# State rows of a streaming convolution moved through small contiguous tiles, and one buffer of the norm's mean in place of two

## The chip, the cores and the metric

One core of one Trainium2 chip runs the whole program. The metric is the device time of one execution in microseconds (us), as the median of several runs. TensorE does the matrix products, VectorE and GpSimd the elementwise work, ScalarE activations and copies, and all transfers between HBM and on-chip memory (SBUF) are issued on SyncE, whose queue the profile calls SPq. TensorE writes to PSUM banks.

## What is computed

Two layers of a streaming encoder, in float32, on 512 prompt frames and 64 frames of a running stream side by side (T = 576 columns, 1,024 features). The part that the change touches is the convolution branch of each layer and the norms. The reference, cut:

```python
def conv_mixer(u, conv_state, conv_w, conv_b, ln_g, ln_b):
    full = jnp.concatenate([conv_state.astype(u.dtype), u], axis=1)
    y = lax.conv_general_dilated(full, conv_w[:, None, :], ..., feature_group_count=C_CONV) + conv_b
    y = jax.nn.silu(layer_norm(y, ln_g, ln_b))
    return y, full[:, -(CONV_WIDTH - 1):]       # the last 30 rows are the new state, an output
...
    h = x @ w_in
    a, g, q, k, v, qi, ki, wi = jnp.split(h, points, axis=-1)
    u = a * jax.nn.sigmoid(g)
    conv_out, new_conv = conv_mixer(u, conv_state, conv_w, conv_b, cln_g, cln_b)
    ...                                         # rope, indexer scores, top-k, attention
    mix = jnp.concatenate([conv_out, attn_out], axis=-1) @ w_o
    x = layer_norm(ALPHA * x + mix, ln1_g, ln1_b)
    gate, up = jnp.split(x @ w_gate_up, 2, axis=-1)
    x = layer_norm(ALPHA * x + (jax.nn.silu(gate) * up) @ w_down, ln2_g, ln2_b)
```

The state goes in for the running stream (`state_conv`), and out for both groups (`new_conv_p`, `new_conv_s`).

## The kernel before, in words

Features lie on the 128 partitions, frames along the free dimension, in two halves of 288 columns. Each weight tile is loaded (`raw`, two buffers), split by ScalarE into a high part (`whi`) and by VectorE or GpSimd into a low part (`wlo`), and a product is three float32r matmuls per block (`products`, `weight`, line 443). 

A layer runs: the products of the convolution's gate and value, the indexer queries and keys with their rotary embedding (`rope`: ScalarE copies the product out of PSUM into `rope_h`, four transfers swap the half heads into `rope_s`, VectorE and GpSimd multiply, VectorE adds), the scores and a top-k by repeated max and replace on VectorE, then keys, values and queries, attention over five query tiles, the convolution's norm, the output projection with its norm, and the feed-forward part with its norm.

The convolution works on four units of 128 channels (`glu(c, ...)`, line 720, c = 0 to 3). The unit's input `u` is a tile of 128 partitions x 8 phases x 80 columns, frame t at phase t mod 8: in each phase 4 columns of zeros, 64 of the prompt, 4 of the old state (from `I_S`) and 8 of the running stream. `glu` clears the zeros on GpSimd, loads the state columns from `st[l, c]` straight into `u`, lets VectorE write gate times value, and stores two pieces of 4 columns per phase to `conv_p` and `conv_s`. The tensors in HBM hold 128 x 8 x 4 numbers without gaps; in `u` each run of 4 numbers (16 B) is followed by a gap. Then `convolve(c)` (line 654) stores all of `u` to a scratch tensor in HBM (`ud<-u`), loads it back with phases on partitions (`v<-ud`, 8 transfers of 16 partitions), builds the tap matrices on GpSimd (`taps`), runs 80 matmuls, and `convolved` (line 679) sends the result back in the same manner (`yd<-y`, `c<-yd`). Units 0 and 1 are made at the head of the layer, units 2 and 3 after the scores.

A norm (`Sums.norm`, line 551) is done for each half of the columns: sums over features on TensorE, then ScalarE spreads the negated mean (`nmu`) and the inverse deviation (`rstd`) over the partitions, VectorE adds and multiplies for eight blocks. Both tiles come from `tmp` (line 421) with two buffers. The tail of the attention's last query tile uses the tag `nmu` too (`ptn`, line 949).

The order of the work is not that of the program text. Every operation is first recorded with a priority, and a planner (`schedule`, line 253) then lays out the whole program as a list on a modelled clock: of the ready operations of an engine it takes the one of lowest priority number, buffers are handed out and freed on that clock, and each engine's instructions, those of the DMA-issuing queue too, stand in that order on the chip, where an instruction that waits holds all behind it. The planner's model prices a transfer by bytes alone, at 360 bytes a nanosecond after a fixed delay, and does not know the size of its pieces; a transfer is issued only when the modelled backlog of DMA is under 3 us. A GpSimd copy of n columns is priced at 0.15 us and 0.0033 us a column. `convolve(c)` has priority CONV + 1000 c, ahead of what comes later in the layer.

```python
            nc.sync.dma_start(u[:, :, I_S:I_S + PADS], ins["st"][l, c])            # line 723
            nc.sync.dma_start(outs["conv_p"][l, c], u[:, :, I_S - PADS:I_S])       # line 731
            nc.sync.dma_start(outs["conv_s"][l, c], u[:, :, CIN - PADS:])          # line 732
```

Of the kernel before, what the change touches and what calls it, by code (L numbers as in the profile page):

```python
# [11 lines left out]
F32 = mybir.dt.float32  # L12
# [5 lines left out]
P = 128  # L18
# [5 lines left out]
HT = T // 2  # L24
# [25 lines left out]
PH = 8  # L50
CB = P // PH
PADS = 32 // PH
CIN = (NP + NS) // PH + 2 * PADS
COUT = CIN - PADS
CJ = 40 // PH
I_S = NP // PH + PADS
# [309 lines left out]
def stream_step(ctx, tc, ins, outs):  # L366
    ctx.enter_context(tc.nc.allow_low_precision(reason="float32r parts"))
    nc = Plan(tc)
# [5 lines left out]
    small = nc.pool(ctx, "small", 4)  # L374
# [28 lines left out]
    def f(x):  # L403
        return x.bitcast(F32)
# [3 lines left out]
    def bank(name, tag="b"):  # L408
        return pb.tile([P, 512], F32, tag=tag, name=name, bufs=BANKS[tag])
# [11 lines left out]
    def tmp(name, tag, n=T, bufs=2):  # L421
        return work.tile([P, n], F32, tag=tag, name=name, bufs=bufs)
# [103 lines left out]
    class Sums:  # L526
# [23 lines left out]

        def norm(self, prm, og, ob, h, last):
            x = lambda k: X[:, k, H[h]]
            nmu, rstd = dst = [tmp(x, x, HT) for x in ("nmu", "rstd")]
            mo = Moments(self.s1[:, H[h]], self.s2[:, H[h]], D, HT, 3, dst)
            mo.stats()
            mo.spread(0)
            mo.spread(1)
            for k in range(KD):
                nc.vector.tensor_add(x(k), x(k), nmu)
                nc.vector.tensor_mul(x(k), x(k), rstd)  # L560
                nc.scalar.activation(x(k), x(k), AF.Identity, scale=prm[:, og + k:og + k + 1],
                                     bias=prm[:, ob + k:ob + k + 1])
                if last:
                    nc.sync.dma_start(outs["y"][:, k, H[h]], x(k))
                else:
                    nc.scalar.activation(XH[:, k, H[h]], x(k), AF.Copy)
                    nc.vector.tensor_sub(XL[:, k, H[h]], x(k), f(XH[:, k, H[h]]))
# [75 lines left out]
    def layer(l):  # L643
# [10 lines left out]
        def convolve(c):  # L654
            wv = slot.tile([P, PH, CJ * PH], F32, tag="wv", name="wv")
            nc.sync.dma_start(wv, ins["cw"][l, c])
            v = slot.tile([P, PH, CIN], F32, tag=f"c{c}", name=f"v{c}")
            ud = dram.tile([P, PH, CIN], F32, tag="ud", name="ud")
            nc.sync.dma_start(ud, us[c])
            for q in range(PH):  # L660
                nc.sync.dma_start(v[q * CB:(q + 1) * CB], ud[:, q, :].rearrange("(b c) t -> c b t", c=CB))
            ps = wide("conv")
            for b in range(PH):
                sw = tmp("taps", "tap", CJ * P)
                shape = [P, CJ * PH, CB]
                nc.gpsimd.tensor_mul(sw.rearrange("p (a b) -> p a b", b=CB), eyes.unsqueeze(1).to_broadcast(shape),
                                     wv[:, b, :].unsqueeze(2).to_broadcast(shape))
                o = b % 4 * COUT
                for j in range(CJ):
                    nc.tensor.matmul(ps[:, b // 4, o:o + COUT], sw[:, j * P:(j + 1) * P], v[:, b, j:j + COUT],  # L670
                                     start=(j == 0), stop=(j == CJ - 1))
            y = slot.tile([P, PH, COUT], F32, tag=f"u{c}", name=f"y{c}")
            for h in range(2):
                nc.vector.tensor_add(y[:, 4 * h:4 * h + 4, :], ps[:, h, :4 * COUT].rearrange("p (b t) -> p b t", b=4),
                                     prm[0][:, O_CB + c * PH + 4 * h:O_CB + c * PH + 4 * h + 4].unsqueeze(2)
                                     .to_broadcast([P, 4, COUT]))
            convolved(c, y)
# [42 lines left out]
        def glu(c, pg, pa):  # L720
            u = slot.tile([P, PH, CIN], F32, tag=f"u{c}", name=f"u{c}")
            nc.gpsimd.memset(u[:, :, 0:PADS], 0.0)
            nc.sync.dma_start(u[:, :, I_S:I_S + PADS], ins["st"][l, c])
            sg = tmp("sg", "sg")
            for h in range(2):
                nc.scalar.activation(sg[:, H[h]], pg[h][:, :HT], AF.Sigmoid)
            for i, h, a, n in ((PADS, 0, 0, HT), (PADS + HT // PH, 1, HT, NP - HT), (I_S + PADS, 1, NP, NS)):
                step = lambda x: x.rearrange("p (t s) -> p t s", s=PH)
                nc.vector.tensor_mul(u[:, :, i:i + n // PH].rearrange("p s t -> p t s"),
                                     step(pa[h][:, a - h * HT:a - h * HT + n]), step(sg[:, a:a + n]))  # L730
            nc.sync.dma_start(outs["conv_p"][l, c], u[:, :, I_S - PADS:I_S])
            nc.sync.dma_start(outs["conv_s"][l, c], u[:, :, CIN - PADS:])
            us.append(u)
            with at(base + CONV + 1000 * c):
                convolve(c)

# [200 lines left out]
        def values(t, u, pr):  # L937
            s = (t + 1) * P if t < 4 else PAST + NS
            sums, _, o = state_[t]
            pt = tmp("pt", "pt", CC)  # L940
            pp = bank("pp", "p")
            nb = min(t + 1, 4)
            for b in range(nb):
                nc.tensor.transpose(pp[:, b * P:(b + 1) * P], pr[:, b * P:(b + 1) * P], ident)
            nc.scalar.activation(pt[:, :nb * P], pp[:, :nb * P], AF.Copy)
            if t == 4:
                pn = bank("pp", "p")
                nc.tensor.transpose(pn[:NS, :P], pr[:, PAST:s], ident)
                ptn = tmp("ptn", "nmu", HT)[:, :P]
                nc.scalar.activation(ptn[:NS], pn[:NS, :P], AF.Copy)  # L950
            d = HD if t < 4 else P
            if u % 4 == 0:
                state_["po"] = bank("po")
            pv = state_["po"][:, (u % 4) * d:(u % 4 + 1) * d]
            gd = slice(u // 4 * HD, (u // 4 + 1) * HD) if t < 4 else slice(0, P)
            for b in range(nb):
                nc.tensor.matmul(pv, pt[:, b * P:(b + 1) * P], (vt if t < 4 else vp)[:, b, gd],
                                 start=(b == 0), stop=(b == t))
            if t == 4:
                nc.tensor.matmul(pv, ptn[:NS], vt[:NS, 4, :], start=False, stop=True)  # L960
            if u % 4 != 3:
                return
            po = state_["po"]
            rs = small.tile([P, 4], F32, tag="rs", name="rs", bufs=2)
            nc.vector.reciprocal(rs, sums[:, u - 3:u + 1])
            if t < 4:
                g = u // 4
                nc.vector.tensor_mul(
                    o[:, g * 256:(g + 1) * 256].rearrange("p (b e d) -> p e b d", b=2, e=2),
                    po[:, :4 * HD].rearrange("p (e b d) -> p e b d", e=2, d=HD),  # L970
                    rs.rearrange("p (e b) -> p e b", e=2).unsqueeze(3).to_broadcast([P, 2, 2, HD]))
                if g == 0:
                    return
                n, no = P, 4
            else:
                po = po.rearrange("p (u g d) -> p u g d", g=2, d=HD)
                for g in range(2):
                    nc.vector.tensor_mul(
                        o[:, g * P:(g + 1) * P].rearrange("p (u d) -> p u d", u=2), po[:, 2 * g:2 * g + 2, g, :],
                        rs[:, 2 * g:2 * g + 2].unsqueeze(2).to_broadcast([P, 2, HD]))  # L980
                n, no = NS, 2
            pm = bank("otr")
            for i in range(no):
                nc.tensor.transpose(pm[:, i * P:(i + 1) * P], o[:, i * P:(i + 1) * P], ident)
            src = pm[:, :4 * n].rearrange("p (i q) -> p i q", i=4)
            hi, lo = XH[:, 4:8, t * P:t * P + n], XL[:, 4:8, t * P:t * P + n]
            nc.scalar.activation(hi, src, AF.Copy)
            nc.vector.tensor_sub(lo, src, f(hi))

        def attend(ts):  # L990
            units = [(t, u) for t in ts for u in range(NH if t < 4 else NH // 2)]
            ahead = []
            for t, u in units:
                ahead.append((t, u, logits(t, u)))
                if len(ahead) > 2:
                    values(*ahead.pop(0))
            for x in ahead:
                values(*x)
# [9 lines left out]
        nmu, rstd = [tmp(x, "tap", UW)[:, :CWID] for x in ("cnmu", "crstd")]  # L1008
# [143 lines left out]
        for part, nf in enumerate(PARTS):  # L1152
# [35 lines left out]
            for j in range(j0, nf):  # L1188
                s = Seven(l, f0 + j, ops)
# [13 lines left out]
            if part < len(PARTS) - 1:  # L1203
                for m in range(KD):
                    ps = products([weight(ins[f"w_d{part}"][l, m], nf * P)], hs)[0]
                    for h in range(2):
                        x = X[:, m, H[h]]
# [115 lines left out]
```

## Time and profile before

| | |
|---|---|
| median of 3 runs | 1572.07 us (1569.68 to 1573.81) |
| profiled execution, its own time | 1578.27 us |
| its span, first to last instruction | 1576.5 us |
| TensorE busy | 1466.2 us (93%) |
| VectorE busy | 1096.8 us (70%) |
| ScalarE busy | 721.0 us (46%) |
| GpSimd busy | 484.3 us (31%) |
| mean granted clock of TensorE | 0.926 of full speed |
| DMA packets | 87,712, of them 49,441 under 512 B |

Busy time is the time in which an engine ran instructions; the rest it waited. Names as `ud<-u` read "written from read". All rows of the trace stand under one line of the code (362), that of the helper that issues the planned list, so operations are told apart by their tiles. A wait is put down to what ended it.

### The profile page before, as it was taken

Reading aid. Unit: us, or ns where it says so; the run is one execution under the profiler, and the core shown is the slowest. Engines: PE = TensorE matmul, PEld = TensorE weight load, DVE = VectorE, ACT = ScalarE, POOL = GpSimd, SP = SyncE. Lnnn points to the kernel's source line nnn. Section 1 sums busy time; section 2 is a strip of 40 time slices with the busy share of each in tenths; the row PEclk is TensorE's granted clock in tenths of the full one; section 3 lists DMA queues with packets and bytes.
Section 4 is the critical chain, followed back from the end, with each engine's and each line's share of the span. In section 5 each row is a group of like instructions: output and inputs, shape, how many; then the busy total and the mean of one; then the engine's idle time right before and its main releaser. Section 6 shows DMA issues by size and latency. Waiting matters only on the chain.

```text
span 1576.5 us, 26565 instructions
## 1 busy us (share of the span) xinstructions
PE 1466.2 (93%) x10246; PEld 1427.4 (91%) x10246; DVE 1096.8 (70%) x2040; ACT 721.0 (46%) x1421; POOL 484.3 (31%) x413
## 2 busy tenths in 40 slices
PE   5799899898999999999996998989989999999996
PEld 5789888898899999999995988979979999999996
DVE  3359878456868668577764989764586785775875
ACT  3334344643635435346453434446364452552643
POOL 1030456333213203122611316533431141230343
PEclk9979959698999999999998997877989999999997
DMA  6625411011132222223327362200112222232221
GB/s 190 121 76 78 118 55 37 14 51 45 54 107 91 88 82 97 90 92 94 99 43 139 73 107 69 68 16 28 55 43 85 101 95 93 81 98 91 78 71 61
DMA packets 87712, 125.12 MB, mean 79 GB/s; under 512 B 49441, under 2 KB 55713, under 8 KB 87585
## 3 DMA queue, kind: packets, MB, share of 16 engines
q1 hardware_dynamic: 87584, 123.42, 28.2%
q8 instruction: 80, 1.31, 0.3%
q14 instruction: 48, 0.39, 0.1%
HBM read 108.81 MB, written 9.21 MB: 75 GB/s over the span
## 4 chain that ended last, share of the span: by engine, by line
PE 74%; DVE 13%; DMA 5%; ACT 3%; SPq 2%; issue 2%; POOL 1%; ACTq 0%; DVEq 0%; POOLq 0%
PE prod L362 30%; PE q L362 16%; PE r L362 8%; PE conv L362 5%; PE c L362 4%; PE po L362 3%; DVE X L362 3%; DMA ud<-u 2%; SPq L362 2%; DVE sel L362 2%; PE qk L362 2%; DVE wlo L362 2%; DVE rope_h L362 2%; PE pp L362 2%; PE dots L362 2%
## 5 line engine op out<-in xcount | busy, mean ns | idle before, releaser
L362 PE MATMUL prod<-XH,whi 128*128 128x288 f32 (+2 forms) x928 | 290.7, 319 | 45.6 <-ACT rope_h L362 25.4
L362 DVE TENSOR_TENSOR wlo<-raw,whi 128x512 fp32r<-128x512 f32 (+2 forms) x199 | 248.4, 1249 | 119.3 <-ACT whi L362 117.3
L362 ACT ACTIVATE whi<-raw 128x1024 fp32r<-128x1024 f32 (+2 forms) x206 | 183.0, 889 | 287.7 <-PE prod L362 174.3
L362 PE MATMUL prod<-XH,wlo 128*128 128x288 f32 (+2 forms) x928 | 290.3, 315 | 7.4 <-DVE wlo L362 7.4
L362 PE MATMUL prod<-XL,whi 128*128 128x288 f32 (+2 forms) x928 | 291.8, 316 | 2.8 <-DVE XL L362 2.7
L362 PEld LDWEIGHTS prod<-XH,whi 128*128 128x128 f32 (+1 forms) x928 | 183.3, 200 | 52.0 <-ACT rope_h L362 27.1
L362 PE MATMUL prod<-hl,whi 128*128 128x288 f32 x704 | 208.0, 296 | 0.2
L362 PE MATMUL prod<-hh,wlo 128*128 128x288 f32 x704 | 207.7, 296 | 0.0
L362 PE MATMUL prod<-hh,whi 128*128 128x288 f32 x704 | 207.0, 295 | 0.0
L362 PEld LDWEIGHTS prod<-XH,wlo 128*128 128x128 f32 (+1 forms) x928 | 182.1, 197 | 10.6 <-DVE wlo L362 8.4
L362 PEld LDWEIGHTS prod<-XL,whi 128*128 128x128 f32 (+1 forms) x928 | 183.8, 198 | 8.2 <-DVE XL L362 6.1
L362 ACT ACTIVATE whi<-s 128x512 fp32r<-128x512 f32 x160 | 96.4, 626 | 134.9 <-PE q L362 101.8
L362 DVE TENSOR_TENSOR wlo<-s,whi 128x512 fp32r<-128x512 f32 x158 | 107.3, 700 | 65.3 <-ACT whi L362 64.3
L362 PE MATMUL q<-XH,wlo 128*128 128x288 f32 x480 | 141.2, 295 | 1.5 <-DVE wlo L362 1.3
L362 PE MATMUL q<-XL,whi 128*128 128x288 f32 x480 | 141.4, 295 | 0.0
L362 PE MATMUL q<-XH,whi 128*128 128x288 f32 x480 | 141.3, 294 | 0.0
L362 PEld LDWEIGHTS prod<-hl,whi 128*128 128x128 f32 x704 | 132.1, 188 | 1.0 <-DVE hl L362 0.7
L362 PEld LDWEIGHTS prod<-hh,wlo 128*128 128x128 f32 x704 | 132.0, 188 | 0.1
L362 PEld LDWEIGHTS prod<-hh,whi 128*128 128x128 f32 x704 | 131.9, 188 | 0.2
L362 POOL TENSOR_TENSOR s<-raw 128x512 f32<-128x512 f32 x28 | 44.9, 1607 | 248.6 <-DVE wlo L362 210.6
L362 POOL TENSOR_TENSOR taps<-eyes,wv 128x640 f32<-128x640 f32 x64 | 87.4, 1369 | 91.1 <-PE conv L362 60.8
L362 DVE TENSOR_TENSOR X<-X,prod 128x288 f32<-128x288 f32 x120 | 53.1, 449 | 86.1 <-PE prod L362 85.5
(195 smaller groups left out, 3537.1 us busy)
## 6 DMA issues: line engine op xcount, KB each, us to landing
raw<-in_w_u SPq DMA_DIRECT2D x44, 512.0 KB, 3.2
raw<-in_w_g SPq DMA_DIRECT2D x44, 512.0 KB, 3.2
raw<-in_w_in SPq DMA_DIRECT2D x36, 512.0 KB, 4.3
raw<-in_w_d SPq DMA_DIRECT2D x48, 384.0 KB, 3.0
raw<-in_w_o SPq DMA_DIRECT2D x16, 512.0 KB, 3.3
raw<-in_w_d SPq DMA_DIRECT2D x16, 256.0 KB, 2.7
rope_s<-rope_h SPq DMA_DIRECT2D x48, 72.0 KB, 2.0
ud<-u SPq DMA_DIRECT2D x8, 320.0 KB, 9.6
```

What stands on the lines that cost most here:

```text
L362: getattr(engine, op.method)(*map(take, op.args), **{k: take(v) for k, v in op.kw.items()})
```

## The change

The state rows are loaded into a small tile `cin` (128 x 32 numbers, one buffer for all units) and copied into `u` by GpSimd; what is stored is first copied by GpSimd out of `u` into a small tile `cout` (two buffers) and stored from there. On both sides of the transfers each partition's 32 numbers are then one run of 128 B. The recording of the two stores also moves behind the line that hands `u` to `convolve`. The mean of the norm gets one buffer instead of two, and with it `ptn`.

```diff
         def norm(self, prm, og, ob, h, last):
-            nmu, rstd = dst = [tmp(x, x, HT) for x in ("nmu", "rstd")]
+            nmu, rstd = dst = [tmp(x, x, HT, n) for x, n in (("nmu", 1), ("rstd", 2))]
...
         def glu(c, pg, pa):
             u = slot.tile([P, PH, CIN], F32, tag=f"u{c}", name=f"u{c}")
             nc.gpsimd.memset(u[:, :, 0:PADS], 0.0)
-            nc.sync.dma_start(u[:, :, I_S:I_S + PADS], ins["st"][l, c])
+            row = small.tile([P, PH * PADS], F32, tag="cin", name="cin", bufs=1)
+            nc.sync.dma_start(row, ins["st"][l, c].rearrange("p s t -> p (s t)"))
+            nc.gpsimd.tensor_copy(u[:, :, I_S:I_S + PADS], row.rearrange("p (s t) -> p s t", s=PH))
...
-            nc.sync.dma_start(outs["conv_p"][l, c], u[:, :, I_S - PADS:I_S])
-            nc.sync.dma_start(outs["conv_s"][l, c], u[:, :, CIN - PADS:])
             us.append(u)
+            for name, i in (("conv_p", I_S - PADS), ("conv_s", CIN - PADS)):
+                row = small.tile([P, PH * PADS], F32, tag="cout", name="cout", bufs=2)
+                nc.gpsimd.tensor_copy(row.rearrange("p (s t) -> p s t", s=PH), u[:, :, i:i + PADS])
+                nc.sync.dma_start(outs[name][l, c].rearrange("p s t -> p (s t)"), row)
             with at(base + CONV + 1000 * c):
                 convolve(c)
...
-                ptn = tmp("ptn", "nmu", HT)[:, :P]
+                ptn = tmp("ptn", "nmu", HT, 1)[:, :P]
```

## Rows read from the trace of the kernel before

**Rows 1.** The page, part 2: forty equal slices (39.4 us each) of the span, counted from 0; busy tenths of TensorE and of the DMA engines.

```profile
PE   5799899898999999999996998989989999999996
...
DMA  6625411011132222223327362200112222232221
```

**Rows 2.** The page: packets of all DMA queues.

```profile
DMA packets 87712, 125.12 MB, mean 79 GB/s; under 512 B 49441, under 2 KB 55713, under 8 KB 87585
```

**Rows 3.** The DMA view: issues by kind, count, KB each, median us from issue to landing.

```profile
raw<-in_w_in SPq DMA_DIRECT2D x36, 512.0 KB, 4.3
...
ud<-u SPq DMA_DIRECT2D x8, 320.0 KB, 9.6
v<-ud SPq DMA_DIRECT2D x64, 40.0 KB, 2.0
yd<-y SPq DMA_DIRECT2D x8, 304.0 KB, 2.2
...
u<-in_st SPq DMA_DIRECT2D x8, 16.0 KB, 2.9
```

**Rows 4.** The timeline of the DMA-issuing queue (SPq), unit 2 of layer 1: start us, us on the queue, operation.

```profile
901.29 0.61 SPq L362 DMA_DIRECT2D out_conv_p<-u  x1
901.99 0.63 SPq L362 DMA_DIRECT2D out_conv_s<-u  x1
```

**Rows 5.** Windows over two neighbouring stretches: stretch, us, then busy us of PE, PEld, DVE, ACT, POOL (with counts), granted clock, DMA share, GB/s.

```profile
901.00:912.00 11.00, 11.00 (x67) 9.92 (x66) 10.61 (x24) 4.92 (x14) 0.00 (x0) 1.00 0.87 71
912.00:921.00 9.00, 9.00 (x68) 8.91 (x67) 8.75 (x20) 4.26 (x7) 2.73 (x3) 1.00 0.37 108
```

**Rows 6.** The timeline of the same queue, units 0 and 3 of layer 0.

```profile
44.80 0.43 SPq L362 DMA_DIRECT2D ud<-u  x1
50.27 0.33 SPq L362 DMA_DIRECT2D raw<-in_w_in  x1
...
55.58 7.85 SPq L362 DMA_DIRECT2D v<-ud  x8
...
64.68 2.52 SPq L362 DMA_DIRECT2D rope_s<-rope_h  x4
...
160.12 2.21 SPq L362 DMA_DIRECT2D v<-ud  x5
162.44 2.48 SPq L362 DMA_DIRECT2D rope_s<-rope_h  x4
```

**Rows 7.** The timeline of ScalarE in layer 0: in brackets the idle time before and what ended it.

```profile
62.04 1.06 ACT L362 ACTIVATE whi<-raw 128x1024 fp32r<-128x1024 f32 x1 [6.30 <-DMA raw<-in_w_in]
```

**Rows 8.** Waits of TensorE from 52 to 100 us: us in total, times, longest.

```profile
PE prod L362 <- ACT rope_h L362: 9.4, 2, 5.8
```

**Rows 9.** The timeline of the DMA-issuing queue, units 0 and 1 of layer 1.

```profile
819.30 0.92 SPq L362 DMA_DIRECT2D out_conv_p<-u  x1
...
841.60 0.32 SPq L362 DMA_DIRECT2D v<-ud  x1
```

**Rows 10.** Waits of TensorE from 810 to 880 us.

```profile
PE prod L362 <- ACT rope_h L362: 8.0, 2, 6.7
PE dots L362 <- DMA rope_s<-rope_h: 5.8, 1, 5.8
```

**Rows 11.** Windows of layer 0, columns as in rows 5: a stretch with waits, the making of units 0 and 1, that of units 2 and 3.

```profile
60.00:110.00 50.00, 37.42 (x197) 35.09 (x198) 28.43 (x41) 18.35 (x39) 16.59 (x12) 0.78 0.43 114
...
40.00:60.00 20.00, 19.98 (x126) 18.94 (x124) 6.08 (x9) 4.19 (x6) 0.00 (x0) 1.00 0.69 88
...
120.00:160.00 40.00, 40.00 (x274) 38.30 (x273) 38.50 (x97) 17.63 (x37) 3.79 (x5) 1.00 0.59 75
```

**Rows 12.** The timeline of VectorE before the keys' rope in layer 0 and in layer 1.

```profile
168.49 0.76 DVE L362 TENSOR_TENSOR rope_h<-rope_h,cos 128x576 f32<-128x576 f32 x1 [7.69 <-DMA rope_s<-rope_h]
...
940.10 0.76 DVE L362 TENSOR_TENSOR rope_h<-rope_h,cos 128x576 f32<-128x576 f32 x1 [6.27 <-DMA rope_s<-rope_h]
```

**Rows 13.** The timeline of the DMA-issuing queue at the start.

```profile
10.04 1.41 SPq L362 DMA_DIRECT2D u<-in_st  x2
...
17.84 0.83 SPq L362 DMA_DIRECT2D raw<-in_w_in  x2
```

**Rows 14.** A group of GpSimd by form: count | busy us, mean ns | idle before.

```profile
L362 POOL CAST qi<-bias 128x64 fp32r<-128x64 f32 x16 | 4.9, 352 | 1.0 <-PE prod L362 1.0
```

**Rows 15.** The timelines of VectorE (the same multiply twice) and of GpSimd (the multiply beside the first).

```profile
189.60 1.54 DVE L362 TENSOR_TENSOR rope_h<-rope_h,cos 128x576 f32<-128x576 f32 x1
...
196.85 0.76 DVE L362 TENSOR_TENSOR rope_h<-rope_h,cos 128x576 f32<-128x576 f32 x1
...
189.09 1.43 POOL L362 TENSOR_TENSOR rope_s<-rope_s,sin 128x576 f32<-128x576 f32 x1
```

**Rows 16.** The last norm of layer 1: VectorE's last uses of the first half's mean, ScalarE's write of the second half's.

```profile
1557.42 0.82 DVE L362 TENSOR_TENSOR X<-X,nmu 128x288 f32<-128x288 f32 x2
...
1565.85 0.41 ACT L362 ACTIVATE nmu<-spread 128x288 f32<-128x288 f32 x1 [1.25 <-PE spread L362]
```

**Rows 17.** The transposed tail of the attention of the last query tile, layer 0: TensorE's read of one unit's, ScalarE's write of the next unit's.

```profile
323.52 0.49 PE L362 MATMUL po<-vt,ptn 64*128 64x128 f32 x2
...
326.06 0.27 ACT L362 ACTIVATE ptn<-pp 64x128 f32<-64x128 f32 x1 [0.77 <-PE pp L362]
```

**Rows 18.** Waits of GpSimd: us in total, times, longest.

```profile
POOL taps L362 <- PE conv L362: 60.8, 41, 5.8
```

## The prediction

> **What bounds the kernel now.** I read the forty slices first, counted from 0 and 39.4 us each: TensorE is at 9 tenths in most, so what can be won is the time in which it waits or runs at its lower clock. The feed-forward slices (11 to 18) are full, with the DMA engines at 2 or 3 tenths. Slices 1 and 21, early in the two layers, have TensorE at 7 and 6 tenths and the DMA engines at 6 and 7 [rows 1]. Then the DMA view: of 87,712 packets 49,441 are under 512 B [rows 2], and among the issues one stands out. Storing the conv input to scratch (ud<-u, 320 KB) takes 9.6 us to land, the same kind of store after the convolution (yd<-y, 304 KB) 2.2 us [rows 3]. What differs is that ud stands behind the two state stores of 16 KB. It is pieces, not bytes, that cost: by the code each state transfer is 128 partitions x 8 phases x 16 B, 1,024 pieces.
>
> What one store costs comes from two neighbouring stretches [rows 5]. From 901 to 912 us, with two stores in it [rows 4], DMA is busy 0.87 x 11 = 9.6 us for 71 GB/s x 11 us = 0.78 MB; from 912 to 921, with none, 0.37 x 9 = 3.3 us for 0.97 MB, or 3.4 us a MB. At that rate 0.78 MB needs 2.7 us, so two stores take 6.9 us, 3.45 us each, 54 ns a piece on each of 16 engines.
>
> Who waits is seen on the DMA queue, which is one, in order. Layer 0: ud goes out at 44.80 and v<-ud can only follow at 55.58; the weights issued at 50.27 reach ScalarE at 62.04, and the first query's rope swap stands behind the v loads until 64.68 [rows 6]. ScalarE, 6.30 us idle before those weights came [rows 7], copies the query products out of PSUM only after them, and TensorE gets its banks that late: 9.4 us of waits for rope_h [rows 8]. Layer 1 has all four stores of two units ahead of ud (819.30 on the queue, and v<-ud first at 841.60) [rows 9]; TensorE waits 8.0 us for rope_h and 5.8 us for the keys' swap [rows 10].
>
> **The change part by part.**
> (a) Stores through rows. Pieces per store fall from 1,024 to 128, at 54 ns x 8 = 0.43 us of the engines instead of 3.45. And ud no longer stands behind them: it needs only u, the row stores need a GpSimd copy first. I take yd's 2.2 us for ud's landing. Then in layer 0 v<-ud could start near 48, weights of 50.27 land in about 4.3 us (the median of their kind [rows 3]) instead of 11.8, and all 9.4 us of TensorE's wait go. **Term 1: 9.4.** In layer 1 likewise 8.0 + 5.8: **term 2: 13.8.**
> (b) The later units (2 and 3) are stored when TensorE is full (40.00 of 40 us in layer 0 [rows 11]), so their delays cost nothing there, but the keys' rope swap comes next on the queue. At 160.12 the v loads of unit 3, held back until ud landed, go out, and the swap is put between them at 162.44 [rows 6]; VectorE, at 38.5 of 40 us the busiest engine beside TensorE, stands for it 7.69 us, and in layer 1 6.27 us [rows 12]. With ud 7 us sooner the v loads are gone before the swap is due. **Terms 3 and 4: 7.7 and 6.3.** Late next is VectorE's top-k itself.
> (c) State rows in. The strided load lands in 2.9 us [rows 3] and has no one waiting, as u is needed much later; its cover is the first two products. New is that one buffer of the row tile serves all four units, so the second unit's load waits for the first one's copy, and a waiting load holds the queue in which the third weight tile stands (17.84, the first state loads being at 10.04 [rows 13]). Bounds: a gain of 1.3 us (four issues near 0.7 us down to the 0.33 of a weight load [rows 6, 13], rounded down), a loss of three links of 2.9 + 0.4 us = 9.9. I take a loss of 2.0, nearer the gain, since the order is laid out with that landing in mind and three of the loads can come later.
> (d) GpSimd copies: 24 of 128x32. Nearest row: a cast of 128x64, 352 ns [rows 14]; 0.35 us taken, 8.4 us in all, on an engine idle (0.00) at units 0 and 1 and busy 3.79 of 40 us at 2 and 3 [rows 11]. A copy can also hold VectorE: the same multiply takes 0.76 us alone and 1.54 us beside GpSimd's [rows 15]. That counts where VectorE is full, at units 2 and 3: 8 copies x 0.35 = 2.8 us, between 0 and 8.4. The Trainium skill, GPSIMD Engine Reference, Specifications, says that GpSimd shares its SBUF interfaces with VectorE, with contention for VectorE operations that read two SBUF inputs or run in a two-port mode. If by that rule every one of the 24 copies held such an operation for its length, 8.4 us would go instead of 2.8, and the sum below would be 23.9; the rows show it for one multiply beside another, and of a copy nothing.
> (e) One buffer of the mean: nothing. In the last norm the second half's mean is written at 1565.85, and the first half's last reads ran from 1557.42 for 0.82 us: 7.6 us of slack [rows 16]. The other user of the buffer writes at 326.06 what was last read by 324.0 [rows 17]. Without that slack it would cost a wait of its length at four norms.
> (f) What does not come back: the keys' swap in layer 1 is a round trip, covered by two query products only if everything else is on time. I keep half of its 5.8 us: 2.9.
>
> Sum: 9.4 + 13.8 + 7.7 + 6.3 = 37.2, less 2.0, 2.8 and 2.9: **29.5 us**. The profiled execution took 1578.27 us (span 1576.5 and 1.8 around it), 6.2 above the median of 1572.07; it would become 1548.8, and against the median that is 1542.6, so **1543**. Bounds: with no debits 37.2; if TensorE also keeps its 2.4 GHz where it now drops toward 1.2 after the waits (in layer 0 mean clock 0.78 over 37.4 busy us [rows 11]) another 0.22 x 37.4 = 8.2. That is a gain of 45: 1527. At the other end term 4 and little else, 8 us: 1564.
>
> **The rivals.**
> *Given back to VectorE.* The score and top-k chain on VectorE runs from the keys to the selection, 38.5 of 40 us busy [rows 11]; if it sets the end of the attention stretch, what TensorE wins before it is lost again and only terms 3 and 4 count, 14.0: 1558. Against it: the chain starts with the keys' rope, which moves too.
> *The rows are still small.* If what costs is a store under some size, and not the count of pieces, 128 B is no better than 16 B and nothing moves: 1572. For it: all these packets are under 512 B. Against it: v<-ud moves 40 KB in pieces of 320 B, also below, and lands in 2.0 us [rows 3]. The Trainium skill, DMA: Bandwidth & Descriptors, Specifications, sets 512 B as the least transfer for full rate, below which the engine reads, modifies and writes; by that rule alone these rows gain nothing.
> *GpSimd holds the queue (slower).* Place: the row stores stand in the one queue, ahead of weights and swaps, and wait for copies that stand on GpSimd behind a taps product that waits for TensorE's convolution. Such waits come 41 times, 60.8 us in all, the longest 5.8 [rows 18]. At 5.8 for each of eight units: 46.4 against the 37.2 won, 1581. It decides from 4.7 us a unit. Against it: GpSimd stands nearly idle where the units are made [rows 11].
>
> **How the numbers follow.** A measurement can tell about 0.3%, 4.7 us, from no change. The forecast has 0.66, all faster. VectorE's share 0.21, of it 0.02 within 0.3%. Small rows 0.06, the same. GpSimd's hold 0.07, of it 0.06 slower and 0.01 the same. So faster 0.85, same 0.09, slower 0.06. The range 1527 to 1564 leaves out the last two rivals (0.13) and about 0.06 of the tails of the first two.
>
> **What would show it.** Right: ud<-u lands in 2 to 4 us, the waits of TensorE for rope_h early in both layers are gone or under 2 us, VectorE's 7.69 and 6.27 us before the keys' rope too, the DMA share in slices 1 and 21 falls by half, packets drop by 24 x 896 = 21,504, norms as before. Wrong: row stores that land late or wait long for GpSimd, weights late at the start (the third weight tile issued after 20 us instead of 17.84), or the same waits of TensorE named after VectorE.

## The result, and the profile after

| | before | after |
|---|---|---|
| median of the runs | 1572.07 us | 1515.39 us (1508.94 to 1524.12, 4 runs) |
| profiled execution, its own time | 1578.27 us | 1524.12 us |
| its span | 1576.5 us | 1522.4 us |
| mean granted clock of TensorE | 0.926 | 0.939 |

The ratio is 0.9644 (95% interval 0.9593 to 0.9695): 56.7 us less, where 29.5 were forecast and 45 was the end of the range. The direction was right, the forecast about half of what came. Medians here and below are of all runs of a kernel; the ratios leave out one run each of e3, e6 and e10, which was longer at a lower granted clock. The two profiled executions, which the rows below come from, differ by 54.1 us.

The page after, part 2: busy tenths of TensorE and of the DMA engines in forty slices; packets.

```profile
PE   6999999998999999999998998999899999999996
...
DMA  5614220011222322223234241101112222222221
...
DMA packets 66207, 125.12 MB, mean 82 GB/s; under 512 B 27936, under 2 KB 34208, under 8 KB 66080
```

Slices 1 and 21, which had TensorE at 7 and 6 tenths and DMA at 6 and 7 [rows 1], now have TensorE at 9 and 8 tenths and DMA at 6 and 4 (the stretches lie a little earlier now). Packets fell from 87,712 [rows 2] by 21,505; 21,504 were forecast.

The DMA view after, columns as in rows 3:

```profile
ud<-u SPq DMA_DIRECT2D x8, 320.0 KB, 2.9
v<-ud SPq DMA_DIRECT2D x64, 40.0 KB, 2.8
...
cin<-in_st SPq DMA_DIRECT2D x8, 16.0 KB, 2.3
out_conv_p<-cout SPq DMA_DIRECT2D x8, 16.0 KB, 2.3
out_conv_s<-cout SPq DMA_DIRECT2D x8, 16.0 KB, 1.8
```

`ud<-u` lands in 2.9 us instead of 9.6, and the state stores themselves in 2.3 and 1.8 us (before 8.0 and 9.6). The queue in layer 0 shows the same; start us, us on the queue, operation:

```profile
37.22 0.33 SPq L362 DMA_DIRECT2D ud<-u  x1
38.34 0.34 SPq L362 DMA_DIRECT2D out_conv_p<-cout  x1
...
40.38 0.80 SPq L362 DMA_DIRECT2D v<-ud  x2
...
48.10 2.52 SPq L362 DMA_DIRECT2D rope_s<-rope_h  x4
```

From `ud<-u` to the first `v<-ud` it is 3.2 us (10.8 before [rows 6]), and the first swap of the half heads goes out 10.9 us after `ud<-u` (19.9 before). TensorE's waits from 40 to 100 us after (us in total, times, longest):

```profile
PE dots L362 <- DVE qi L362: 2.7, 1, 2.7
PE dots L362 <- ACT ki L362: 1.1, 1, 1.1
PE dots L362 <- ACT relu L362: 0.8, 1, 0.8
```

The 9.4 us for `rope_h` of [rows 8] are gone, and so are the 8.0 and 5.8 us of layer 1 [rows 10]; over the whole span TensorE waited 25.4 us for `rope_h` before, and after no longer at all. The wait of VectorE before the keys' rope, 7.69 and 6.27 us [rows 12], is now 0.3 us in layer 0 (and 0.6 us in layer 1), put down to GpSimd:

```profile
DVE rope_h L362 <- POOL rope_s L362: 0.3, 1, 0.3
```

To see where 54.1 us went I cut both executions into seven stretches at the same events: start; first write of `u` in layer 0; the scores on the new keys; the convolution's norm; and the same three in layer 1; end. Columns as in rows 5. Before:

```profile
0.00:28.50 28.50, 11.68 (x59) 11.17 (x60) 11.31 (x21) 14.00 (x24) 6.27 (x24) 0.97 0.79 233
28.50:127.80 99.30, 86.30 (x518) 82.44 (x517) 49.11 (x86) 32.96 (x66) 18.43 (x14) 0.87 0.42 95
127.80:281.90 154.10, 138.74 (x912) 131.76 (x911) 129.74 (x312) 63.09 (x148) 69.15 (x55) 0.84 0.33 68
281.90:809.70 527.80, 516.51 (x3753) 507.40 (x3752) 366.26 (x620) 260.71 (x492) 155.47 (x134) 0.96 0.24 77
809.70:896.30 86.60, 70.82 (x441) 66.88 (x440) 51.48 (x87) 34.24 (x71) 19.36 (x14) 0.90 0.51 99
896.30:1051.50 155.20, 138.71 (x939) 131.76 (x937) 131.06 (x316) 62.55 (x146) 65.85 (x53) 0.88 0.33 68
1051.50:1576.50 525.00, 503.43 (x3635) 495.98 (x3634) 357.81 (x603) 253.47 (x476) 149.73 (x119) 0.94 0.22 74
```

After:

```profile
0.00:24.10 24.10, 10.09 (x63) 9.81 (x63) 11.27 (x20) 13.88 (x24) 8.09 (x27) 1.00 0.85 286
24.10:105.20 81.10, 76.51 (x494) 73.57 (x493) 50.16 (x82) 32.17 (x65) 21.42 (x19) 0.94 0.39 114
105.20:248.10 142.90, 136.35 (x939) 128.59 (x937) 129.35 (x317) 63.61 (x149) 67.84 (x59) 0.90 0.26 74
248.10:775.50 527.40, 516.04 (x3748) 508.34 (x3747) 368.13 (x620) 260.89 (x493) 160.91 (x138) 0.96 0.23 77
775.50:848.20 72.70, 67.62 (x437) 64.54 (x436) 53.06 (x88) 34.30 (x71) 20.15 (x18) 0.95 0.42 119
848.20:996.20 148.00, 140.29 (x942) 133.63 (x941) 131.76 (x315) 63.04 (x146) 68.86 (x57) 0.85 0.25 71
996.20:1522.40 526.20, 502.17 (x3636) 494.79 (x3634) 360.88 (x603) 253.51 (x476) 148.76 (x119) 0.95 0.22 73
```

The two long stretches (4 and 7) stand still: 1052.8 and 1053.6 us together. The start is 4.4 us shorter, and the four stretches 2, 3, 5 and 6, in which units are made, scored and attended, fell from 495.2 to 444.7 us. Their TensorE idle time (length less busy) fell from 60.6 to 23.9 us, **36.7 us**, and their busy time, for the same matmuls, from 434.6 to 420.8, **13.8 us**: the granted clock rose in stretches 2, 3 and 5 (0.87, 0.84 and 0.90 before, 0.94, 0.90 and 0.95 after), and in stretch 6 it was lower after (0.88, 0.85). Of the 13.8 us, 12.2 are in layer 0 and 1.6 in layer 1.

### The profile page after: what moved, and what is told of

Same layout as the page of the kernel before. It is cut to its first block, busy times and chain, and to the rows that moved or that the text cites. A ratio compares the mean times of both kernels' runs of the same rounds, so it can differ in the third digit from the quotient of the medians.

```text
span 1522.4 us, 26598 instructions
## 1 busy us (share of the span) xinstructions
PE 1449.1 (95%) x10246; PEld 1413.3 (93%) x10246; DVE 1104.6 (73%) x2040; ACT 721.4 (47%) x1421; POOL 496.0 (33%) x437
## 4 chain that ended last, share of the span: by engine, by line
PE 78%; DVE 13%; ACT 3%; issue 2%; DMA 2%; POOL 1%; SPq 1%; ACTq 0%; DVEq 0%; POOLq 0%
PE prod L362 33%; PE q L362 16%; PE r L362 8%; PE conv L362 5%; PE c L362 4%; PE po L362 3%; DVE X L362 2%; DVE sel L362 2%; DVE rope_h L362 2%; PE qk L362 2%; PE dots L362 2%; PE pp L362 2%; PE spread L362 2%; DVE wlo L362 2%; PE stats L362 1%
## 5 line engine op out<-in xcount | busy, mean ns | idle before, releaser
L362 PE MATMUL prod<-XH,whi 128*128 128x288 f32 (+2 forms) x928 | 282.9, 310 | 18.5 <-ACT whi L362 16.4
L362 PE MATMUL prod<-XH,wlo 128*128 128x288 f32 (+2 forms) x928 | 285.0, 310 | 7.4 <-DVE wlo L362 7.4
L362 PE MATMUL prod<-XL,whi 128*128 128x288 f32 (+2 forms) x928 | 285.9, 310 | 2.9 <-DVE XL L362 2.8
L362 PEld LDWEIGHTS prod<-XH,whi 128*128 128x128 f32 (+1 forms) x928 | 177.6, 193 | 22.5 <-ACT whi L362 17.3
L362 PEld LDWEIGHTS prod<-XH,wlo 128*128 128x128 f32 (+1 forms) x928 | 177.9, 192 | 10.4 <-DVE wlo L362 8.3
L362 PEld LDWEIGHTS prod<-XL,whi 128*128 128x128 f32 (+1 forms) x928 | 178.9, 193 | 7.7 <-DVE XL L362 5.8
L362 POOL TENSOR_TENSOR taps<-eyes,wv 128x640 f32<-128x640 f32 x64 | 86.9, 1361 | 71.0 <-PE conv L362 57.2
```

Source lines behind the costliest of these rows:

```text
L362: getattr(engine, op.method)(*map(take, op.args), **{k: take(v) for k, v in op.kw.items()})
```

## The experiments

A transfer is made of pieces: a piece is a run of bytes with no gap in it, neither where it is read nor where it is written. The theory: stores in pieces of 16 B are slow, and hold `ud`, the weights and the swaps behind them; the stores, not the loads, the copies or the norm, make the gain. The rivals: it is only that `ud` no longer stands behind them; the loads at the start; and, later, that what costs is the number of the pieces, or anything under 512 B. In the table, "four" are stretches 2, 3, 5 and 6 of each kernel's profile, "start" is stretch 1, all in us; the ratio is that to the kernel before on the same chip (its median there was 1572 to 1582).

| kernel | median | ratio (interval) | start | four: length | busy | idle | conv_p, conv_s land in |
|---|---|---|---|---|---|---|---|
| before | 1572.07 | 1 | 28.5 | 495.2 | 434.6 | 60.6 | 8.0, 9.6 |
| after | 1515.39 | 0.9644 (0.9593, 0.9695) | 24.1 | 444.7 | 420.8 | 23.9 | 2.3, 1.8 |
| e1_gap_both | 1561.55 | 0.9873 (0.9807, 0.9940) | 24.2 | 484.4 | 425.5 | 58.9 | 8.8, 9.7 |
| e2_gap_in | 1524.76 | 0.9634 (0.9553, 0.9715) | 24.5 | 442.9 | 416.5 | 26.4 | 2.5, 1.8 |
| e3_gap_out | 1555.61 | 0.9810 (0.9727, 0.9892) | 23.6 | 484.9 | 427.7 | 57.2 | 8.2, 9.7 |
| e4_ud_first | 1556.34 | 0.9842 (0.9769, 0.9915) | 28.4 | 473.0 | 424.4 | 48.6 | 6.4, 9.2 |
| e5_rows_out | 1523.94 | 0.9647 (0.9604, 0.9690) | 28.8 | 446.0 | 418.3 | 27.7 | 2.4, 1.8 |
| e6_rows_in | 1571.66 | 0.9961 (0.9929, 0.9993) | 24.0 | | | | 7.8, 10.2 |
| e7_cin4 | 1519.13 | 0.9613 (0.9575, 0.9650) | 26.6 | 437.1 | 411.7 | 25.4 | 2.5, 1.9 |
| e8_no_stores | 1520.30 | 0.9621 (0.9586, 0.9655) | 24.4 | 442.5 | 419.5 | 23.0 | |
| e9_gap32 | 1514.89 | 0.9569 (0.9519, 0.9619) | 24.2 | 442.1 | 415.2 | 26.9 | 2.6, 2.2 |
| e10_gap64 | 1518.87 | 0.9576 (0.9504, 0.9648) | | | | | 2.5, 1.9 |
| e11_changed | 1513.36 | 0.9550 (0.9488, 0.9612) | 24.2 | 445.9 | 418.8 | 27.1 | 2.4, 1.9 |
| e12_gap16_one | 1533.26 | 0.9725 (0.9698, 0.9752) | 24.9 | 461.3 | 422.3 | 39.0 | 6.4, 5.9 |

Cells of e6 and e10 are empty because in each profile one stretch has a long fall of the granted clock (stretch 3 of e6, 0.76; stretch 6 of e10, 0.77); their idle time, 60.1 and 23.2 us, is like that of the kernels before and after. e8 has no such stores.

**The pieces back, the order kept (e1, e2, e3).** The row tiles get gaps, so that copies, buffers and the order of all engines stay those of the changed kernel, and only the transfers go in pieces of 16 B again. e1 does both of the following, e2 the first alone, e3 the second alone:

```diff
-            row = small.tile([P, PH * PADS], F32, tag="cin", name="cin", bufs=1)
-            nc.sync.dma_start(row, ins["st"][l, c].rearrange("p s t -> p (s t)"))
+            row = small.tile([P, PH, 2 * PADS], F32, tag="cin", name="cin", bufs=1)[:, :, :PADS]
+            nc.sync.dma_start(row, ins["st"][l, c])
...
-                row = small.tile([P, PH * PADS], F32, tag="cout", name="cout", bufs=2)
+                row = small.tile([P, PH, 2 * PADS], F32, tag="cout", name="cout", bufs=2)[:, :, :PADS]
...
-                nc.sync.dma_start(outs[name][l, c].rearrange("p s t -> p (s t)"), row)
+                nc.sync.dma_start(outs[name][l, c], row)
```

> The changed kernel with both row tiles laid out with gaps (128 x 8 x 8, of which 4 columns are used), so that each state transfer is again 1,024 pieces of 16 B; every engine's instructions stand in the same order as in the changed kernel. Theory P (the pieces cost): most of the 56.7 us come back, 1550 to 1572 us, DMA packets back at about 87,700, and 4 us or less of the gain stays for ud standing ahead of the stores. Rival O (the planner's new order gave the gain, not the pieces): 1510 to 1525 us.

> The changed kernel with gaps in the load's row tile alone (8 loads of 1,024 pieces), same order. Theory P with the start as the missing term: the 7.6 us won before the first store of ud come back, 1522 to 1525 us, and the third weight tile lands near 24 us again instead of 19. Rival O (the start was won by the order of the loads on the queue): 1515 us, within 3 us of the changed kernel.

> The changed kernel with gaps in the stores' row tiles alone (16 stores of 1,024 pieces), same order. Theory P: 40 to 47 us come back, 1555 to 1562 us, with waits of TensorE for rope_h after units 0 and 1 again. Rival Q (only what stands ahead of ud matters, and here ud goes first): 1515 to 1530 us. Rival O: 1515 us.

Measured: e2 is not told apart from the changed kernel; on the same chip e3 is 30.9 us and e1 36.8 us slower than e2. So pieces of 16 B cost in stores, and in these loads nothing that can be told. The loss is less than the 40 to 47 us expected, and e1 keeps 20 us of the gain where 4 or less were expected. And the start stays short with small pieces in the loads (24.5 us in e2), which the expectation had wrong. The DMA view of e3:

```profile
ud<-u SPq DMA_DIRECT2D x8, 320.0 KB, 6.0
...
out_conv_p<-cout SPq DMA_DIRECT2D x8, 16.0 KB, 8.2
out_conv_s<-cout SPq DMA_DIRECT2D x8, 16.0 KB, 9.7
```

TensorE's waits of e3 over the whole span (25.4 us for the same before, none after):

```profile
PE prod L362 <- ACT rope_h L362: 22.8, 6, 11.2
```

With `ud` issued first, the waits for `rope_h` are back all the same, because what stands behind the stores now is the second unit's `ud`, the `v` loads and the swaps. The queue of e3 in layer 1, the first unit's `ud` and its `v` loads:

```profile
799.07 0.33 SPq L362 DMA_DIRECT2D ud<-u  x1
...
805.88 0.80 SPq L362 DMA_DIRECT2D v<-ud  x2
...
820.10 6.20 SPq L362 DMA_DIRECT2D v<-ud  x4
```

and the same in the changed kernel:

```profile
785.23 0.77 SPq L362 DMA_DIRECT2D ud<-u  x1
...
788.32 0.84 SPq L362 DMA_DIRECT2D v<-ud  x2
...
794.70 2.00 SPq L362 DMA_DIRECT2D v<-ud  x4
```

The first loads go out 6.8 us after `ud` against 3.1, the four in the middle 21.0 against 9.5, for the same order.

**The order alone (e4).** In the kernel before, with no row tiles, the two stores are recorded behind the convolution. On the chip's queue `ud` then goes first for units 0 and 1, and between the two stores for units 2 and 3:

```diff
-            nc.sync.dma_start(outs["conv_p"][l, c], u[:, :, I_S - PADS:I_S])
-            nc.sync.dma_start(outs["conv_s"][l, c], u[:, :, CIN - PADS:])
...
+            with at(base + CONV + 1000 * c + 2):
+                nc.sync.dma_start(outs["conv_p"][l, c], u[:, :, I_S - PADS:I_S])
+                nc.sync.dma_start(outs["conv_s"][l, c], u[:, :, CIN - PADS:])
```

> The kernel before, with its strided stores recorded behind the whole of convolve(c) instead of ahead, at a priority just behind ud; no row tiles, no copies. Rival Q (ud behind the stores is the cost): 1530 to 1545 us. Theory P (the stores hold whatever stands behind them, weights and swaps too): 1560 to 1575 us.

Measured: 0.9842, 25 us less (13 to 37), between the two ranges expected. `ud` still lands in 7.8 us, and TensorE still waits 16.8 us for `rope_h`. So the order is worth something with pieces of 16 B still there. That these 25 us and e3's 31 for the size add up to the 56 of the whole change is in part chance: each is known to 12 us or worse, and of the 36.7 us of idle time the order alone takes 12.0 in e4, and the changed kernel's order with 16 B stores 3.4 in e3.

**One half of the change at a time (e5, e6).** Both have the one buffer of the mean. e5 has the stores through `cout` and the strided loads of before; e6 the loads through `cin` and the strided stores of before. The edits against the changed kernel, e5 and then e6:

```diff
-            row = small.tile([P, PH * PADS], F32, tag="cin", name="cin", bufs=1)
-            nc.sync.dma_start(row, ins["st"][l, c].rearrange("p s t -> p (s t)"))
-            nc.gpsimd.tensor_copy(u[:, :, I_S:I_S + PADS], row.rearrange("p (s t) -> p s t", s=PH))
+            nc.sync.dma_start(u[:, :, I_S:I_S + PADS], ins["st"][l, c])
```

```diff
+            nc.sync.dma_start(outs["conv_p"][l, c], u[:, :, I_S - PADS:I_S])
+            nc.sync.dma_start(outs["conv_s"][l, c], u[:, :, CIN - PADS:])
             us.append(u)
-            for name, i in (("conv_p", I_S - PADS), ("conv_s", CIN - PADS)):
...
```

> The kernel before with the stores through row tiles alone (and one buffer of the mean); the state loads stay strided and early. Theory S (the start is won by the load part of the change, the rest by the stores): the first write of u stays near 28.5 us, all later stretches are as short as in the changed kernel, a ratio to before of 0.967 to 0.970. Rival R (the planner's re-ordering as a whole, started by any edit, gives some of it): 0.975 to 0.985.

> The kernel before with the state loads through the one row tile alone (and one buffer of the mean); the stores stay strided, ahead of ud. Theory S: the first write of u comes 4 to 5 us sooner, near 24 us, nothing else moves, a ratio of 0.995 to 0.998. Rival R: 0.985 to 0.99, as in the run with gaps in both tiles (0.9873).

Measured: the stores alone give 0.9647, all that can be told of the gain; the loads alone 0.9961, some 6 us (1 to 11). The start goes with the loads: 28.8 us in e5, 24.0 in e6.

**The loads' buffer (e7).** Four buffers in place of one in the changed kernel:

```diff
-            row = small.tile([P, PH * PADS], F32, tag="cin", name="cin", bufs=1)
+            row = small.tile([P, PH * PADS], F32, tag="cin", name="cin", bufs=4)
```

> The changed kernel with four buffers of the load's row tile instead of one, so that no load waits for a copy. Theory W (the one buffer wins the start, because its waits spread the loads behind the weights): the first write of u moves back toward 28 us, a ratio of 0.967 to 0.969. Rival X (the waits cost, as the prediction's loss of 2.0 us has it): 1 to 2 us faster than the changed kernel, 0.963. Rival Y (with contiguous rows neither): 0.964.

Measured: not told apart from the changed kernel in time (theory W's 0.967 to 0.969 is missed), but the start tells how the 4.4 us come. The first stretches of e5 (small pieces, loads in pairs) and of e7 (rows, loads in pairs); that of the changed kernel (rows, spaced by the one buffer) stands above:

```profile
0.00:28.80 28.80, 10.52 (x55) 10.01 (x56) 11.22 (x20) 13.94 (x24) 6.29 (x24) 0.93 0.75 229
```

```profile
0.00:26.60 26.60, 11.76 (x66) 11.48 (x67) 11.23 (x20) 13.85 (x24) 8.19 (x28) 1.00 0.78 253
```

28.8, 26.6 and 24.1 us. On the queue four small loads stand ahead of the third weight tile in e5, five in e7, and two after: the wait for the one buffer, which I had priced as a loss, holds the others back behind that tile, and the start is 2.5 us shorter than in e7. The size of the pieces makes about 2.2 us where the loads come in pairs (e5 against e7), and little where they are spaced (24.5 us in e2). In e7 the next stretch is 4.5 us shorter (76.6 against 81.1 us), so the start's gain need not reach the end.

**No stores at all (e8).** The 16 copies and 16 stores of the state are left out of the changed kernel, and these outputs stay unwritten:

```diff
-            for name, i in (("conv_p", I_S - PADS), ("conv_s", CIN - PADS)):
-                row = small.tile([P, PH * PADS], F32, tag="cout", name="cout", bufs=2)
-                nc.gpsimd.tensor_copy(row.rearrange("p (s t) -> p s t", s=PH), u[:, :, i:i + PADS])
-                nc.sync.dma_start(outs[name][l, c].rearrange("p s t -> p (s t)"), row)
```

> The changed kernel without the row copies and stores of the new state (16 copies, 16 stores; these outputs are left unwritten). It prices what the stores still cost. Theory P: 0.43 us of the DMA engines a store and copies beside other work, so 0 to 4 us faster than the changed kernel, 0.962 to 0.9644. Rival V (copies hold VectorE, the 2.8 to 8.4 us of the prediction): 0.959 to 0.9625.

Measured: 0.9621, inside the interval of the changed kernel, and where the ranges of theory P and rival V overlap. Stores through rows and their copies cost nothing that can be told; 2.8 us would be too little to tell.

**Number or size of the pieces (e9 to e12).** e9 stores in 512 pieces of 32 B, e10 in 256 of 64 B, the order unchanged; e11 is the changed kernel beside them; e12 leaves `conv_p` in 1,024 pieces of 16 B and stores `conv_s` in rows, so that a unit has 1,152 pieces, nearly e9's 1,024. The edit of e9 (the grouping is 4 phases in e10) and of e12:

```diff
-                row = small.tile([P, PH * PADS], F32, tag="cout", name="cout", bufs=2)
+                row = small.tile([P, PH // 2, 4 * PADS], F32, tag="cout", name="cout", bufs=2)[:, :, :2 * PADS]
...
+                nc.sync.dma_start(outs[name][l, c].rearrange("p (a b) t -> p a (b t)", b=2), row)
```

```diff
+                row = small.tile([P, PH * 2 * PADS], F32, tag="cout", name="cout", bufs=2)
+                row = (row.rearrange("p (s t) -> p s t", s=PH)[:, :, :PADS] if name == "conv_p" else
+                       row[:, :PH * PADS].rearrange("p (s t) -> p s t", s=PH))
...
+                nc.sync.dma_start(outs[name][l, c], row)
```

> The changed kernel with the stores' row tiles in four runs of 32 B a partition: 512 pieces a store, the order of every engine unchanged. Theory N (each piece has its price): 384 of the 896 extra pieces, 0.43 of the 26 us that the run with 1,024 pieces lost, 11 us, a ratio to before near 0.971; the two stores of a unit land in about half the time (4 to 5 us). Rival M (a run under some size is slow as such): as with 16 B, 0.981. Rival K (only past a number of pieces in flight does the queue stall): under 3 us lost, 0.966 or less.

> The same with two runs of 64 B: 256 pieces a store. Theory N: 128 of 896, 0.14 of 26 us, 4 us, 0.967. Rival M: 0.981. Rival K: nothing, 0.9644.

> The changed kernel itself on the same chip as the two before it, as their base: 0.9644, and a span of its stretches that tells what scatter there is between two profiles of one order: the first five stretches within 1 us, the last two within 7.

> The changed kernel with the prompt's state stored in 1,024 pieces of 16 B and the stream's state in contiguous rows: 8 stores in place of 16 have small pieces, and a unit sends 1,152 pieces, about as many as with 32 B in both (1,024), order unchanged. Theory Z (pieces of 16 B are slow to write, whatever their number): about half of what 16 B in both lost (26 us between 0.981 and 0.964), a ratio of 0.967 to 0.975, and the state stores land in 4 to 6 us. Rival K (the number in flight): as with 32 B, within 3 us of the changed kernel, 0.955 to 0.966, landing under 3 us.

Measured: e9 and e10 are not told apart from e11. e12, on another chip, has a ratio of 0.9725, against 0.955 to 0.958 for these three and 0.9644 for the changed kernel's first runs: 13 to 28 us slower. Its four stretches, 461.3 us, are 15 to 24 us longer than those of the seven kernels without 16 B stores (437.1 to 446.0). The DMA views of e9 and of e12:

```profile
ud<-u SPq DMA_DIRECT2D x8, 320.0 KB, 3.0
...
out_conv_p<-cout SPq DMA_DIRECT2D x8, 16.0 KB, 2.6
out_conv_s<-cout SPq DMA_DIRECT2D x8, 16.0 KB, 2.2
```

```profile
ud<-u SPq DMA_DIRECT2D x8, 320.0 KB, 5.6
...
out_conv_p<-cout SPq DMA_DIRECT2D x8, 16.0 KB, 6.4
out_conv_s<-cout SPq DMA_DIRECT2D x8, 16.0 KB, 5.9
```

With about the same number of pieces in a unit, `ud` lands in 3.0 us beside pieces of 32 B and in 5.6 beside pieces of 16 B; even `conv_s`, in rows itself, takes 5.9 us behind a `conv_p` of 16 B. So it is the 16 B piece, not the number of pieces in a unit and not a bound at 512 B. Not tried is a bound on the pieces of one store: a store of e9 has 512, the slow ones 1,024.

## Why the prediction was right or wrong

**Waits (terms 1 to 4, and f): right in size.** Stretches 2 and 3 are read together, because some 25 matmuls changed sides of the mark between them. Terms 1 and 3 said 9.4 + 7.7 = 17.1 us; TensorE's idle time in layer 0 fell from 28.4 to 11.1, 17.2 us. Terms 2 and 4 said 13.8 + 6.3 = 20.1, less 2.9 for the round trip; it fell in layer 1 from 32.3 to 12.8, 19.5 us. In stretch 5 alone it fell by 10.7, near 13.8 less 2.9, so the half that I kept for the round trip was about right there; what TensorE waits for in that place after is VectorE (2.6 us for `wtok`, 1.2 for `qi`), no longer the swap. In stretches 3 and 6 it fell by 8.8 us each, more than the 7.7 and 6.3 of VectorE's waits: 8.0 us for `rope_h` went (4.4 and 3.6), and 7.2 us of waits for VectorE's `mx` in the attention, which no term had. All the waits named (rows 8, 10 and 12) are gone, and e3 brings those for `rope_h` back with nothing changed but the stores' pieces. So the rival in which VectorE takes the gain back is out: the idle time won early is not lost later. One thing I looked for did not come: the DMA share of slice 1 is not halved, as the same bytes now move in less time (114 instead of 95 GB/s in stretch 2).

**The clock: the step that failed.** The prediction let the granted clock stand in a bound only, 8.2 us for one stretch of layer 0, and took nothing for it in the sum. It belongs in the sum, and for both layers. Windows before, two of layer 0 in a row, then one more of layer 0 and one of layer 1, show how the waits cost twice:

```profile
72.00:78.00 6.00, 1.36 (x7) 0.92 (x5) 5.18 (x9) 4.23 (x9) 1.13 (x1) 1.00 0.54 148
78.00:84.00 6.00, 4.87 (x13) 4.35 (x14) 3.20 (x7) 3.32 (x8) 0.13 (x1) 0.50 0.52 149
...
176.00:182.00 6.00, 6.00 (x32) 6.00 (x32) 6.00 (x21) 2.29 (x4) 3.85 (x4) 0.64 0.22 49
...
842.00:848.00 6.00, 3.46 (x9) 3.11 (x10) 2.24 (x3) 1.89 (x3) 1.58 (x1) 0.55 0.38 91
```

TensorE ran 1.36 of 6 us, and in the next 6 its granted clock is 0.50, that is 1.2 instead of 2.4 GHz, with 13 matmuls in 4.87 us. In the other two windows, which follow or hold the end of waits for `rope_h` of 4.4 and 6.7 us, it is 0.64 and 0.55. Not every fall is the stores' doing: there is another before from 97 us, behind a wait of 2.0 us for VectorE (clock 0.70 and 0.50), and its like stands after too, behind a gap (3.35 of 6 us) that the stores did not make:

```profile
72.00:78.00 6.00, 3.35 (x27) 2.98 (x25) 5.73 (x8) 1.88 (x5) 4.63 (x3) 1.00 0.45 134
78.00:84.00 6.00, 6.00 (x32) 5.99 (x33) 4.27 (x8) 0.65 (x2) 3.13 (x3) 0.60 0.00 0
84.00:90.00 6.00, 6.00 (x31) 6.00 (x29) 2.67 (x4) 1.96 (x5) 2.33 (x2) 0.55 0.08 27
```

That busy time follows the stores is seen in the table. The four kernels with all stores in 16 B pieces (before, e1, e3, e4) have TensorE busy 424.4 to 434.6 us in the four stretches, mean 428.1; the seven with none (after, e2, e5, e7, e8, e9, e11) 411.7 to 420.8, mean 417.3. That is **10.8 us of busy time** for the same matmuls, on top of the idle time, and the two groups do not overlap; e12, with half of these stores, lies between them (422.3). It is 6.3 us in layer 0 and 4.5 in layer 1. e6 and e10 are left out for the long fall in one stretch, and e10, at 435.3, would make the groups overlap. The 13.8 of the pair of profiles holds some scatter beside it: kernels of one group differ by 9 to 10 us.

Why the time fell outside the range can be told in the prediction's terms. The range's end, 37.2 + 8.2 = 45.4 us, is 8.7 short of the 54.1 of the profiles: the clock gave 13.8 where 8.2 were the bound, 5.6 more, and the start gave 4.4 where the bound had nothing; all else is 1.3 less.

**Start (c): wrong in sign.** I took a loss of 2.0 us and let the gain end at 1.3; the start is 4.4 us shorter. I had counted the one buffer's waits as time of the queue, and gave nothing for the loads that they put behind the third weight tile: before four small loads stand ahead of it, after two. It was issued at 15.74 instead of 17.84 and taken by ScalarE 5.2 us sooner; ScalarE before, then after:

```profile
24.39 1.06 ACT L362 ACTIVATE whi<-raw 128x1024 fp32r<-128x1024 f32 x1 [7.17 <-DMA raw<-in_w_in]
...
19.22 1.06 ACT L362 ACTIVATE whi<-raw 128x1024 fp32r<-128x1024 f32 x1 [3.37 <-DMA raw<-in_w_in]
```

**Copies (d): 2.8 us that are not seen.** The 24 copies took 10.6 us of GpSimd, a quarter more than the 8.4 estimated:

```profile
L362 POOL COPY cout<-u 128x32 f32<-128x32 f32 x16 | 7.4, 484 | 44.6 <-DVE u L362 33.8 <-issue 8.4 <-DMA out_conv_p<-cout 2.1
...
L362 POOL COPY u<-cin 128x32 f32<-128x32 f32 x8 | 3.2, 398 | 21.5 <-DMA cin<-in_st 21.5
```

In stretches 3 and 6, where VectorE is full, VectorE was busy 260.8 us before and 261.1 after, and leaving 16 of the copies out (e8) gains nothing that can be told. The Trainium skill, GPSIMD Engine Reference, Specifications, has GpSimd share its SBUF interfaces with VectorE, with contention for VectorE operations that read two SBUF inputs or run in a two-port mode; of these copies no run here shows it. The rival in which the stores hold the queue for GpSimd falls too: in the rows of the queue above the first store goes out 1.1 us after `ud`, and no wait of TensorE for what stands behind it is left.

**One buffer of the mean (e): nothing, as said,** as far as the runs tell. It was not run alone. Stretch 7, with the norms of layer 1, took 525.0 us before and 521.2 in e4, both with two buffers, and 519.3 to 526.2 in the kernels with one.

**The price in (a): right for the pieces removed, wrong as a rule.** 54 ns a piece was measured on 16 B pieces and stood for "pieces, not bytes". It made 3.45 less 0.43, 3.0 us of the DMA engines a store. By part 3 of the pages, the packets on the queue of SyncE took (share times span) 444 to 455 us of the 16 engines' time in the four kernels with all stores in 16 B pieces and 385 to 410 in after, e2, e5, e7, e9, e10 and e11; the means differ by 44 us, 2.8 us a store. With half as many pieces a price per piece would leave half of the delay, but the stores of e9 land in 2.6 and 2.2 us, within 0.4 of those of the rows. The price belongs to the 16 B piece. The rival of small rows, in which anything under 512 B is slow, is out with the 56.7 us. The Trainium skill, DMA: Bandwidth & Descriptors, Specifications, sets the least transfer for full rate at 512 B, with a read-modify-write below; here 32, 64 and 128 B stores behave alike (e9, e10, e11), so 512 B is not where this cost begins. The Trainium skill, Collectives: The Full Stack, Rules for kernel authors, asks that the buffers of collectives be aligned to 32 B, to avoid a read-modify-write in the hardware. The plain stores here agree with a bound between 16 and 32 B, but whether a read-modify-write is the cause no run shows.

The sum as it should have been, from the rows: 37.2 less 2.9 of waits, 10.8 of clock and 4.4 of the start make 49.5 us, against 54.1 in the profiles and 56.7 in the medians. The rest, 5 to 7 us, is not settled; profiles of one group differ by as much.

## What to carry to other kernels

Look in the DMA view for a transfer that lands late without being large, and then at what stands ahead of it in the queue: a store that goes in pieces of 16 B, because its tile on the chip has gaps between them, is the thing to look for, and a copy into a contiguous tile (or just runs of 32 B, as in e9) is a cheap cure. A wait of TensorE that goes can be worth more than its length, if the granted clock in the windows behind it is below 1: take the busy time that comes back into the sum, not into the bound. The order of the transfers alone was worth 25 us (e4) and the size of their pieces 31 (e3 against e2), each to 12 us or worse, so each is tried by itself.

## What the runs showed of the hardware

- Stores of 16 KB in pieces of 16 B land in 6.4 to 10.2 us, and delay what follows them on the queue; in pieces of 32, 64 or 128 B they land in 1.8 to 2.6 us (rows of 128 B behind a 16 B store in 5.9, e12). Loads of the same 16 KB in pieces of 16 B land in 3.1 us against 2.3 and cost no time that can be told (e2, 0.9634). Why a 16 B store is so slow stays open: by the code the pieces lie apart where they are read, on the chip, and next to each other where they are written, in HBM.
- Where TensorE's idle time in the four stretches is 31 to 37 us less (after against before, e1 and e3 against the mean of the seven), its busy time for the same matmuls is 8 to 14 us less too.
- Small loads ahead of a weight tile delay it: with four or five ahead of it ScalarE takes it at 24.4 us (before), 24.7 (e5) and 22.4 (e7), with two at 19.2 (after) and 20.4 (e2).
